# Down projection sums scaled by r and added to h in the output, in place of h divided by r beforehand

## The chip, the cores and the metric

The kernel runs on one core of one Trainium2 chip. The core has TensorE (matrix products; PE and, for its weight loads, PEld in the profile), VectorE (DVE), ScalarE (ACT), GpSimd (POOL) and SyncE (SP). SP and GpSimd issue the DMAs here, each from its own queue in order. The metric is the device time of one execution in microseconds (us).

## The reference

The reference is one decoder layer: 512 tokens behind 16 learned ones, width 2048. What matters here is its second half.

```python
        h = h + o @ w_out[l]

        n2 = _rmsnorm(h, g_ffn[l])
        h = h + (jax.nn.silu(n2 @ w_gate[l]) * (n2 @ w_up[l])) @ w_down[l]

    return h[:, N_META:]
```

`_rmsnorm` multiplies each token with r = 1/sqrt(mean(h*h) + EPS) and each channel with a gain. The inner width of the gate, up and down products is 5632. Since r is one number for each token, it may be applied after a product instead of before: silu(r * (h g) @ w_gate) and r * ((h g) @ w_up), and then the down projection's sum too may take r as a whole.

## The kernel before

All tiles are transposed: 128 channels on the partitions, 512 tokens along the free dimension. The layer runs in stages: input projection, attention and convolution (to about 650 us), output projection with the residual (to 800), gate and up products (800 to 1660), down projection (1660 to the end).

A product in 32-bit precision is made of three passes over operands split into a high and a low part. In the last two stages `pair_product` computes two output tiles for both halves of the tokens at once by a scheme of Strassen's kind: seven block products (numbered 0 to 6) into three PSUM tiles y, z, x (lines 702 to 704). Their weights are prepared by `prepare_pair` under high priority: four weight blocks are loaded by SP (line 591), VectorE adds them up (lines 616, 623, 650), ScalarE casts each of the seven to its high part (609), and VectorE subtracts for the low part (610). Between block products, partial sums are moved out of PSUM: ScalarE copies x, z and x to `sides` (727, 729, 731), and VectorE combines them (733, 737, 740). A PSUM tile can be written again when it was moved out.

**Gate and up.** The loop over f (44 channel tiles of the inner width) runs one `pair_product` each, which gives g1 and u1, and then `gate`: g1 takes r on VectorE (905; r is `r_h`, the tile `acc_h`), silu on ScalarE (906), and the product with u1, which has no r, is made on VectorE, for even f in lines 909 and 910, for odd f in 915 to 918. The results are split (183, 184) and stored to DRAM tiles `fd` through GpSimd's queue (897).

**h and r.** Since u1 lacks r, the down projection's sums lack it as well, and the kernel keeps h / r beside them. The residual stage stores the 16 tiles of h into DRAM tiles `hs[j]`, named hd (line 865). `h_scale` computes r in the first pair, with most of its element-wise work on GpSimd, and `h_inv` = 1/r (499). After the odd f up to 31 a round of `h_over` runs on GpSimd: load a tile of h, multiply it by `h_inv`, store it back (944 to 946).

**Down.** The inner width is split into four chunks of 4, 6, 6 and 6 double tiles. In chunk 0, four pair products make four output tiles each; in chunks 1 to 3, eight make two each. The activations of a chunk are loaded from `fd` into rings through GpSimd's queue (932). In chunks 0 to 2 the sums c1 and c2 are added to `hs` in DRAM by an accumulating DMA of GpSimd's queue:

```python
        gp.dma_start(two(hs[j]), c[:, :, n * T2 :][:, :, :T2], accum_op=ALU.add)
```

for which ScalarE first copies the last block x into c1 (982, 1015). In chunk 3 (`end`) the tiles of `hs` are loaded into `hh` (1000), the sums are added, and the total takes r: c2 on GpSimd (1006, 1007), the two halves of c1 on VectorE (1009 to 1012). SP stores the result to `out` (1008, 1013).

**Order.** A scheduling framework turns this program into one in-order queue for each engine. It simulates the engines with a cost model and takes, of the work that is ready, what stands first in the program; the preparation of weights goes ahead by its high priority. It also sets the waits between queues, from the tiles and tensors that are read and written.

Of the kernel before, what the change touches and what calls it, by code (L numbers as in the profile page):

```python
# [22 lines left out]
KT = D // P  # L23
FT = FF // P

CHUNKS = (4, 6, 6, 6)
# [7 lines left out]
def hybrid_layer(ctx: ExitStack, tc: tile.TileContext, xT, w_in, w_out, w_gu, w_down, vecs, out):  # L34
# [265 lines left out]
    def two(t):  # L300
        return t.rearrange("p (a b) -> p a b", a=2)
# [181 lines left out]
    for h in range(HEADS):  # L483
        head(h)

    def token_scale(acc, dst, count, name, work, inv=None, eng=ve):

        sh, sl, v, y, t = work
        split(sh, sl, acc, eng)
        ps = small(f"ss_{name}")
        pe.matmul(ps, ones_r, sh, start=True, stop=False)
        pe.matmul(ps, ones_r, sl, start=False, stop=True)
        ve.tensor_scalar(v, ps, 1.0 / count, EPS, ALU.mult, ALU.add)
        rsqrt(dst, v, SEQ, y, t, eng)
        if inv is not None:
            eng.tensor_tensor(inv, v, dst, ALU.mult)


    def scale_a():
# [241 lines left out]

    dram = ctx.enter_context(tc.tile_pool(name="dram", bufs=1, space=bass.MemoryType.DRAM))
    fpool = open_pool("fpool", side="right")
    hbuf = open_pool("hbuf", side="right")

    def slots(pool, dt, m, n, name, **kw):

        c = 2 * m * n * T2
        t = pool.tile([P, c + 64], dt, name=name, **kw)
        t = t[:, 4 : 4 + c].rearrange("p (s a k t) -> p s a k t", s=m, a=2, k=n)
        return [t[:, s] for s in range(m)]
# [22 lines left out]
        token_scale(acc_c, acc_c, 1024, "c", w)  # L779

    after(3, scale_c)
    hs = {}
    for i, j in enumerate(OUT_TILES):
        hj = wide_tmp("h", bufs=2)
        gp.dma_start(hj, xT[j][:, META:])
# [75 lines left out]
                    gp.dma_start(fx[s][:, :, k], st[:, :, n])  # L861
        if i < KT - 1:
            square_sum(acc_h, hj, i == 0, wide_tmp("s"))
        hd = dram.tile([P, SEQ], F32, name=f"hd{j}")
        (gp if i < KT - 1 else nc.sync).dma_start(hd, hj)
        hs[j] = hd
    assert not waiting
    acts = [acts[s] for s in range(7)]
    hbuf.release()
# [2 lines left out]
    xyz = open_pool("xyz", 2, space=PSUM)  # L872
    sm = open_pool("sm2", 1, space=PSUM)
    apool = open_pool("apool")
    h_inv = apool.tile([P, SEQ], F32, name="h_inv")

    def h_scale():
        w = apool.tile([P, 5, SEQ], F32R, tag="s5", name="work_r")
        a, b = apool.tile([P, 2, SEQ], F32, tag="odd", name="work_a"), apool.tile([P, SEQ], F32, tag="even", name="work_b")
        with tc.high_priority(1 << 20):  # L880
            token_scale(acc_h, acc_h, D, "h", (w[:, 0], w[:, 1], a[:, 0], a[:, 1], b), h_inv, gp)

    r_h = two(acc_h)

# [16 lines left out]
    even = [None]  # L901

    def gate(f, g1, u1, x):
        sc.copy(g1[:, 1], x)
        ve.tensor_tensor(g1, g1, r_h, ALU.mult)
        sc.activation(g1, g1, AF.Silu)
        if f % 2 == 0:
            even[0] = even_f = apool.tile([P, 3, T2], F32, tag="even", name=f"even{f}")
            ve.tensor_tensor(even_f[:, 0:3:2], g1, u1, ALU.mult)
            ve.tensor_tensor(even_f[:, 1], even_f[:, 0], even_f[:, 2], ALU.subtract)  # L910
# [23 lines left out]
    for f in range(FT):  # L934
        g1 = apool.tile([P, 2, T2], F32, tag="c1", name=f"g{f}")
        u1 = apool.tile([P, 2, T2], F32, tag="c2", name=f"u{f}")
        x = pair_product(acts, g1, u1, None if f else h_scale)
        if f < FT - 1:
            gate(f, g1, u1, x)
        if f % 2 and f // 2 < KT:  # L940

            j = f // 2
            h_over = apool.tile([P, SEQ], F32, tag="odd", name=f"h_over{j}")
            gp.dma_start(h_over, hs[j])
            gp.tensor_tensor(h_over, h_over, h_inv, ALU.mult)
            gp.dma_start(hs[j], h_over)
        if f == 2 * CHUNKS[0] + 1:
            load_acts(0, 0)
    fpool.release()
# [14 lines left out]
    new_places(6)  # L964
    new_places(7)

    def add_down(j, c, n):
        gp.dma_start(two(hs[j]), c[:, :, n * T2 :][:, :, :T2], accum_op=ALU.add)

    for j in range(KT // 4):  # L970
        for s in range(2 * j - 2, 2 * j) if j else ():
            load_acts(1, s)
        c1, c2 = ((d, d_first)[j % 2][:, m : m + 2] for m in (0, 2))
        x = pair_product([rings[0, s] for s in range(7)], c1, c2)
        if j == KT // 4 - 1:
            first.release()
            rings_p[1] = open_pool("ring_a", side="right")
            for i in (1, 3, 4, 5):
                new_places(i)
            pad(rings_p[1], 160)  # L980
            load_acts(1, 6)
        sc.copy(c1[:, 1], x)
        for n in range(2):
            add_down(4 * j + 2 * n + 1, c2, n)
        for n in range(2):
            add_down(4 * j + 2 * n, c1, n)
    for c in range(1, len(CHUNKS)):
        end = c == len(CHUNKS) - 1
        if end:

            hh = slots(rings_p[1], F32, 1, 6, "hh", tag="ring4")[0]
        for j in range(KT // 2):

            if 1 <= j <= 5:
                load_acts(c + 1, j - 1)
            c1, c2 = (two(d[:, j % 2 * 2 + m]) for m in range(2))
            if end:
                h2 = [hh[:, :, 2 * (j % 3) + m] for m in range(2)]
                for m in (1, 0):
                    gp.dma_start(h2[m], two(hs[2 * j + m]))  # L1000
            x = pair_product([rings[c, s] for s in range(7)], c1, c2)
            if j == KT // 2 - 1:
                for s in (5, 6):
                    load_acts(c + 1, s)
            if end:
                gp.tensor_tensor(c2, c2, h2[1], ALU.add)
                gp.tensor_tensor(c2, c2, r_h, ALU.mult)
                nc.sync.dma_start(two(out[2 * j + 1]), c2)
                ve.tensor_tensor(c1[:, 0], c1[:, 0], h2[0][:, 0], ALU.add)
                ve.tensor_tensor(c1[:, 0], c1[:, 0], r_h[:, 0], ALU.mult)  # L1010
                ve.tensor_tensor(c1[:, 1], x, h2[0][:, 1], ALU.add)
                ve.tensor_tensor(c1[:, 1], c1[:, 1], r_h[:, 1], ALU.mult)
                nc.sync.dma_start(two(out[2 * j]), c1)
            else:
                sc.copy(c1[:, 1], x)
                add_down(2 * j + 1, c2, 0)
                add_down(2 * j, c1, 0)
    rings_p[2].release()
    cpool.release()
    rings_p[1].release()  # L1020
# [58 lines left out]
```

## Time and profile before

| what | value |
|---|---|
| median of 3 runs | 2099.22 us (2098.17 to 2100.97) |
| profiled execution | 2099.6 us |
| its span, first to last instruction | 2097.5 us |
| granted TensorE clock, mean | 0.998 |
| VectorE busy | 1637.8 us (78%) |
| GpSimd busy | 465.5 us (22%) |
| h_over rounds: load, product, store | 16 each; product 1959 ns, mean |
| last chunk on GpSimd, line 1006 | 8 of 1866 ns, mean |
| accumulating DMAs into hd | 48 of 256 KB |

A line of a group gives line, engine, operation, output<-inputs, the tile's shape, the number of them, then busy time and the mean of one in ns, then the idle time ahead of them and what ended it. A line of the waits gives who waited for what: total us, times, longest. A line of the timeline gives start and duration in us, engine, line and operation, and in brackets how long the engine sat idle before it and what it waited for. A row by source line gives how many there were, the minimum, median and maximum in ns, and the first and last start in us. A row of the windows gives the stretch, its length, then the busy us and the number of instructions of PE, PEld, DVE, ACT and POOL, the granted clock, the share of the DMA engines and GB/s.

### The profile page before, as it was taken

To read this page: it belongs to the slowest core of one execution; us is meant where nothing else is said; L and a number is where in the kernel's file an instruction comes from. 1 tells how busy PE (TensorE), PEld (TensorE's weight loads), DVE (VectorE), ACT (ScalarE), POOL (GpSimd) and SP (SyncE) were. 2 spreads that over 40 slices of the span, in tenths; PEclk is the share of its full clock that TensorE was granted. 3 is DMA by queue.
4 is the path that set the end of the run, shared out by engine and by line. 5 is a ranking of instruction groups with operands and counts; after the bars stand their busy time and mean duration, and the time that the engine had idled before them with its cause. 6 is when DMAs were issued, how large, how long until landed. Compare 5 with 4: busy or idle time off the path is not lost.

```text
span 2097.5 us, 39273 instructions
## 1 busy us (share of the span) xinstructions
PE 2064.9 (98%) x16086; PEld 1985.3 (95%) x16086; DVE 1637.8 (78%) x2075; ACT 1018.4 (49%) x1532; POOL 465.5 (22%) x577
## 2 busy tenths in 40 slices
PE   8999999999999998999999999999999999999998
PEld 7999999999998888999999999999999999999998
DVE  8777767533336668899899899899888977778798
ACT  5666666322224434555555555554555544444443
POOL 4111111010104544122122122122011243131322
PEclk9999999999999999999999999999999999999999
DMA  5222222222235666556555565565455899696853
GB/s 174 81 71 81 71 81 72 91 91 91 92 120 156 191 180 227 167 153 204 166 168 176 160 183 174 155 187 163 145 172 166 267 340 343 154 338 158 240 172 111
DMA packets 147795, 342.46 MB, mean 163 GB/s; under 512 B 13136, under 2 KB 62800, under 8 KB 147616
## 3 DMA queue, kind: packets, MB, share of 16 engines
q1 hardware_dynamic: 69472, 216.17, 32.3%
q0 software_dynamic: 78144, 123.79, 21.7%
q8 instruction: 126, 2.06, 0.4%
q14 instruction: 53, 0.43, 0.1%
HBM read 268.60 MB, written 71.30 MB: 162 GB/s over the span
## 4 chain that ended last, share of the span: by engine, by line
PE 78%; DVE 10%; ACT 4%; issue 4%; DMA 2%; POOL 1%; SPq 0%; ACTq 0%; DVEq 0%; POOLq 0%
PE x L702 7%; PE x L704 7%; PE x L703 7%; PE z L702 4%; DVE s L610 4%; PE z L703 4%; PE z L704 4%; PE po L682 3%; PE po L683 3%; PE po L681 3%; ACT s L609 3%; PE y L704 2%; PE y L703 2%; PE y L702 2%; PE pv L169 2%
## 5 line engine op out<-in xcount | busy, mean ns | idle before, releaser
L609 ACT CAST s<-t 128x1024 fp32r<-128x1024 f32 (+1 forms) x288 | 283.2, 983 | 342.5 <-PE z L704 169.2
L610 DVE TENSOR_TENSOR s<-t,s 128x1024 fp32r<-128x1024 f32 (+1 forms) x288 | 334.4, 1161 | 116.6 <-ACT s L609 116.2
L703 PE MATMUL x<-f,s 128*128 128x256 f32 x1408 | 387.5, 275 | 2.3 <-DVE f L184 1.3
L704 PE MATMUL x<-f,s 128*128 128x256 f32 x1408 | 387.4, 275 | 1.7 <-DVE s L610 1.7
L702 PE MATMUL x<-f,s 128*128 128x256 f32 x1408 | 387.4, 275 | 0.2 <-ACT f L183 0.2
L609 ACT CAST s<-b 128x1024 fp32r<-128x1024 f32 (+1 forms) x216 | 212.4, 983 | 156.8 <-PE x L704 151.3
L703 PEld LDWEIGHTS x<-f,s 128*128 128x128 f32 x1408 | 264.3, 188 | 2.7 <-DVE f L184 1.5
L704 PEld LDWEIGHTS x<-f,s 128*128 128x128 f32 x1408 | 264.3, 188 | 1.9 <-DVE s L610 1.9
L702 PEld LDWEIGHTS x<-f,s 128*128 128x128 f32 x1408 | 264.3, 188 | 0.5 <-ACT f L183 0.4
L610 DVE TENSOR_TENSOR s<-b,s 128x1024 fp32r<-128x1024 f32 (+1 forms) x216 | 257.4, 1192 | 2.7 <-ACT s L609 2.2
L138 DVE TENSOR_TENSOR wlo<-raw,whi 128x512 fp32r<-128x512 f32 (+1 forms) x198 | 142.4, 720 | 131.1 <-ACT whi L137 130.5
L897 POOL DMA_DIRECT2D fd<-s x147 | 104.1, 925 | 528.8 <-DVE s L184 527.3
L137 ACT CAST whi<-raw 128x512 fp32r<-128x512 f32 (+1 forms) x198 | 121.3, 614 | 185.4 <-PE pu L171 65.5
L702 PE MATMUL z<-f,s 128*128 128x256 f32 x704 | 195.8, 278 | 7.6 <-ACT sides L729 7.6
L703 PE MATMUL z<-f,s 128*128 128x256 f32 x704 | 193.9, 275 | 0.0
L704 PE MATMUL z<-f,s 128*128 128x256 f32 x704 | 193.9, 275 | 0.0
L616 DVE TENSOR_TENSOR t<-b,b 128x1024 f32<-128x1024 f32 (+1 forms) x144 | 165.5, 1149 | 15.7 <-DMA b<-w_down 11.0
L702 PE MATMUL x<-ring,s 128*128 128x256 f32 x608 | 168.8, 278 | 7.8 <-ACT sides L727 4.0
L704 PE MATMUL x<-ring,s 128*128 128x256 f32 x608 | 167.6, 276 | 0.5 <-DVE s L610 0.5
L703 PE MATMUL x<-ring,s 128*128 128x256 f32 x608 | 167.4, 275 | 0.0
L702 PEld LDWEIGHTS z<-f,s 128*128 128x128 f32 x704 | 132.2, 188 | 10.9 <-ACT sides L729 10.9
L704 PEld LDWEIGHTS z<-f,s 128*128 128x128 f32 x704 | 132.2, 188 | 0.0
(356 smaller groups left out, 5681.0 us busy)
## 6 DMA issues: line engine op xcount, KB each, us to landing
b<-w_gu SPq DMA_DIRECT2D x176, 512.0 KB, 4.0
raw<-w_in SPq DMA_DIRECT2D x92, 512.0 KB, 3.3
fd<-s POOLq DMA_DIRECT2D x147, 256.0 KB, 5.3
b<-w_down SPq DMA_DIRECT2D x96, 384.0 KB, 3.9
ring<-fd POOLq DMA_DIRECT2D x42, 768.0 KB, 15.7
wide<-w_out SPq DMA_DIRECT2D x30, 512.0 KB, 3.8
hd<-d POOLq DMA_DIRECT2D x40, 256.0 KB, 7.5
b<-w_down SPq DMA_DIRECT2D x16, 512.0 KB, 7.7
```

What stands on the lines that cost most here:

```text
L137: sc.copy(hi[:, :c], raw)
L138: ve.tensor_tensor(lo[:, :c], raw, hi[:, :c].bitcast(F32), ALU.subtract)
L609: sc.copy(hi, src)
L610: ve.tensor_tensor(lo, src, hi.bitcast(F32), ALU.subtract)
L616: ve.tensor_tensor(sums[name], a, b, ALU.add)
L681: pe.matmul(ps, hi[:, kk], ah, start=k == 0, stop=False)
L682: pe.matmul(ps, hi[:, kk], al, start=False, stop=False)
L683: pe.matmul(ps, lo[:, kk], ah, start=False, stop=k == 7)
L702: pe.matmul(p, hi[:, kk], act[:, 0, k], start=start and j == k == 0, stop=False, skip_group_check=skip)
L703: pe.matmul(p, hi[:, kk], act[:, 1, k], start=False, stop=False, skip_group_check=skip)
L704: pe.matmul(p, lo[:, kk], act[:, 0, k], start=False, stop=k == n - 1, skip_group_check=skip)
L897: gp.dma_start(fd[c][s][:, :, k], t[:, :, i])
```

## The change

- The residual stage stores h at once into `out[j]`. The DRAM tiles hd, `h_inv` and the sixteen `h_over` rounds are gone.
- In `gate`, u1 takes r on VectorE for the first eight f, which are the activations of chunk 0. The sums of chunk 0 thus have r in them already.
- In chunks 1 to 3 the sums take r on VectorE as they leave `pair_product` (c2 as a whole, c1 in two halves, the second read from PSUM in place of ScalarE's copy), and an accumulating DMA adds them to `out`.
- Only the very last pair is treated otherwise: its two tiles of `out` are loaded, added on VectorE, and stored by SP.
- GpSimd computes nothing in the down projection or for h after r; it issues the DMAs.

```diff
-        if inv is not None:
-            eng.tensor_tensor(inv, v, dst, ALU.mult)
...
-        hd = dram.tile([P, SEQ], F32, name=f"hd{j}")
-        (gp if i < KT - 1 else nc.sync).dma_start(hd, hj)
-        hs[j] = hd
+        (gp if i < KT - 1 else nc.sync).dma_start(out[j], hj)
...
     def gate(f, g1, u1, x):
+        if f < 2 * CHUNKS[0]:
+
+            ve.tensor_tensor(u1, u1, r_h, ALU.mult)
         sc.copy(g1[:, 1], x)
...
-        if f % 2 and f // 2 < KT:
-
-            j = f // 2
-            h_over = apool.tile([P, SEQ], F32, tag="odd", name=f"h_over{j}")
-            gp.dma_start(h_over, hs[j])
-            gp.tensor_tensor(h_over, h_over, h_inv, ALU.mult)
-            gp.dma_start(hs[j], h_over)
...
-    def add_down(j, c, n):
-        gp.dma_start(two(hs[j]), c[:, :, n * T2 :][:, :, :T2], accum_op=ALU.add)
+    def add_down(j, c):
+        gp.dma_start(two(out[j]), c, accum_op=ALU.add)
+
+    def part(c, n):
+        return c[:, :, n * T2 : (n + 1) * T2]
+
+    def down(c1, c2, acts, j, so_far):
+
+        x = pair_product(acts, c1, c2)
+        ve.tensor_tensor(c2, c2, r_h, ALU.mult)
+        if so_far:
+            ve.tensor_tensor(c2, c2, so_far[1], ALU.add)
+            nc.sync.dma_start(two(out[2 * j + 1]), c2)
+        else:
+            add_down(2 * j + 1, c2)
+        for k, src in enumerate((c1[:, 0], x)):
+            ve.tensor_tensor(c1[:, k], src, r_h[:, k], ALU.mult)
+            if so_far:
+                ve.tensor_tensor(c1[:, k], c1[:, k], so_far[0][:, k], ALU.add)
+        if so_far:
+            nc.sync.dma_start(two(out[2 * j]), c1)
+        else:
+            add_down(2 * j, c1)
...
-        for n in range(2):
-            add_down(4 * j + 2 * n + 1, c2, n)
-        for n in range(2):
-            add_down(4 * j + 2 * n, c1, n)
+        for m, c in ((1, c2), (0, c1)):
+            for n in range(2):
+                add_down(4 * j + 2 * n + m, part(c, n))
     for c in range(1, len(CHUNKS)):
-        end = c == len(CHUNKS) - 1
-        if end:
-
-            hh = slots(rings_p[1], F32, 1, 6, "hh", tag="ring4")[0]
         for j in range(KT // 2):
...
-            if end:
-                h2 = [hh[:, :, 2 * (j % 3) + m] for m in range(2)]
-                for m in (1, 0):
-                    gp.dma_start(h2[m], two(hs[2 * j + m]))
-            x = pair_product([rings[c, s] for s in range(7)], c1, c2)
+            so_far = None
+            if c == len(CHUNKS) - 1 and j == KT // 2 - 1:
+
+                hh = slots(rings_p[1], F32, 1, 6, "hh", tag="ring4")[0]
+                so_far = [hh[:, :, n] for n in range(2)]
+                for n in range(2):
+                    gp.dma_start(so_far[n], two(out[2 * j + n]))
+            down(c1, c2, [rings[c, s] for s in range(7)], j, so_far)
...
-            if end:
-                gp.tensor_tensor(c2, c2, h2[1], ALU.add)
-                gp.tensor_tensor(c2, c2, r_h, ALU.mult)
-                nc.sync.dma_start(two(out[2 * j + 1]), c2)
-                ve.tensor_tensor(c1[:, 0], c1[:, 0], h2[0][:, 0], ALU.add)
-                ve.tensor_tensor(c1[:, 0], c1[:, 0], r_h[:, 0], ALU.mult)
-                ve.tensor_tensor(c1[:, 1], x, h2[0][:, 1], ALU.add)
-                ve.tensor_tensor(c1[:, 1], c1[:, 1], r_h[:, 1], ALU.mult)
-                nc.sync.dma_start(two(out[2 * j]), c1)
-            else:
-                sc.copy(c1[:, 1], x)
-                add_down(2 * j + 1, c2, 0)
-                add_down(2 * j, c1, 0)
```

More of the change, by code (lines that the diff above doesn't have):

```diff
@@ L484, in hybrid_layer, with token_scale @@
         head(h)
-    def token_scale(acc, dst, count, name, work, inv=None, eng=ve):
+    def token_scale(acc, dst, count, name, work, eng=ve):
         sh, sl, v, y, t = work
@@ L781, in hybrid_layer @@
     after(3, scale_c)
-    hs = {}
     for i, j in enumerate(OUT_TILES):
@@ L874, in hybrid_layer @@
     apool = open_pool("apool")
-    h_inv = apool.tile([P, SEQ], F32, name="h_inv")
     def h_scale():
@@ L880, in h_scale @@
         with tc.high_priority(1 << 20):
-            token_scale(acc_h, acc_h, D, "h", (w[:, 0], w[:, 1], a[:, 0], a[:, 1], b), h_inv, gp)
+            token_scale(acc_h, acc_h, D, "h", (w[:, 0], w[:, 1], a[:, 0], a[:, 1], b), gp)
     r_h = two(acc_h)
```

## The prediction

> **What bounds the kernel now.** I read the busy line first, then the waits of TensorE stage by stage, then the timeline around each wait.
>
> ```profile
> PE 2064.9 (98%) x16086; PEld 1985.3 (95%) x16086; DVE 1637.8 (78%) x2075; ACT 1018.4 (49%) x1532; POOL 465.5 (22%) x577
> ```
>
> TensorE sets the time, so the change can win only where TensorE stands still because something is late. Two such places repeat. The first is the gate and up stage; these are waits of its window from 860 to 1482 us (total, times, longest):
>
> ```profile
> ACT s L183 <- DVE even L910: 12.2, 11, 1.1
> ...
> PE z L702 <- ACT sides L729: 6.9, 16, 0.4
> ```
>
> Sixteen times TensorE waits for the same copy. How long a pair of products takes there is seen from the copy of line 904, which runs once in each: its number, and its first and last start, in the window 849 to 1470 and then in 1489 to 1640.
>
> ```profile
> L904 ACT COPY g<-x x32: 376/377/378, 850.0 to 1451.5; 128x256 f32<-128x256 f32 x32
> ...
> L904 ACT COPY g<-x x8: 376/377/378, 1490.3 to 1623.6; 128x256 f32<-128x256 f32 x8
> ```
>
> The later window takes 133.3/7 = 19.04 us a pair, with no wait. The earlier one takes 601.5 us for 31 pairs, 11.2 us over 31 x 19.04, and holds 15 of the 16 waits: 0.75 us each. The timeline names the cause. First a pair with the wait:
>
> ```profile
> 873.01 2.20 POOL L945 TENSOR_TENSOR h_over<-h_over,h_inv 128x512 f32<-128x512 f32 x1 [7.39 <-DMA h_over<-hd]
> 873.97 2.33 DVE L610 TENSOR_TENSOR s<-b,s 128x1024 fp32r<-128x1024 f32 x1
> 876.22 0.41 DVE L910 TENSOR_TENSOR even<-even 128x256 f32<-128x256 f32 x1
> 876.67 0.62 ACT L183 CAST s<-even 128x512 fp32r<-128x512 f32 x1 [1.11 <-DVE even L910]
> 877.19 0.37 ACT L729 COPY sides<-z 128x256 f32<-128x256 f32 x1
> 877.61 0.39 PE L702 MATMUL z<-f,s 128*128 128x256 f32 x1 [0.43 <-ACT sides L729]
> ```
>
> Then a pair without GpSimd's product:
>
> ```profile
> 1491.06 0.69 DVE L905 TENSOR_TENSOR g<-g,acc_h 128x512 f32<-128x512 f32 x1
> 1492.32 1.23 DVE L610 TENSOR_TENSOR s<-t,s 128x1024 fp32r<-128x1024 f32 x1 [0.57 <-ACT s L609]
> ...
> 1495.20 1.22 DVE L610 TENSOR_TENSOR s<-b,s 128x1024 fp32r<-128x1024 f32 x1
> 1496.33 0.42 DVE L910 TENSOR_TENSOR even<-even 128x256 f32<-128x256 f32 x1
> ...
> 1497.31 0.37 ACT L729 COPY sides<-z 128x256 f32<-128x256 f32 x1
> ...
> 1498.25 0.28 PE L702 MATMUL z<-f,s 128*128 128x256 f32 x1
> ```
>
> The same subtraction of line 610 takes 2.33 us beside GpSimd's multiplication and 1.22 without it. VectorE is 1.1 us late with line 910, ScalarE stands with line 183 in front of line 729, and TensorE needs line 729 before it may overwrite z. In the calm pair line 729 is done at 1497.68 and needed at 1498.25: 0.57 us of slack.
>
> The second place is the last chunk of the down projection. Its steady pair, and after it one of the chunk before:
>
> ```profile
> 2061.05 0.42 DVE L740 TENSOR_TENSOR d<-y,sides 128x256 f32<-128x256 f32 x1
> 2062.24 1.37 POOL L1007 TENSOR_TENSOR d<-d,acc_h 128x512 f32<-128x512 f32 x1
> 2062.37 2.05 DVE L610 TENSOR_TENSOR s<-t,s 128x768 fp32r<-128x768 f32 x1
> 2064.68 0.95 DVE L650 TENSOR_TENSOR t<-t,b 128x768 f32<-128x768 f32 x1
> 2067.21 0.36 ACT L727 COPY sides<-x 128x256 f32<-128x256 f32 x1
> 2067.63 0.39 PE L702 MATMUL x<-ring,s 128*128 128x256 f32 x1 [0.50 <-ACT sides L727]
> ```
>
> ```profile
> 1940.23 0.42 DVE L740 TENSOR_TENSOR d<-y,sides 128x256 f32<-128x256 f32 x1
> 1941.10 0.96 DVE L610 TENSOR_TENSOR s<-t,s 128x768 fp32r<-128x768 f32 x1 [0.45 <-ACT s L609]
> 1942.09 0.96 DVE L650 TENSOR_TENSOR t<-t,b 128x768 f32<-128x768 f32 x1
> 1944.01 0.96 DVE L610 TENSOR_TENSOR s<-t,s 128x768 fp32r<-128x768 f32 x1 [0.96 <-ACT s L609]
> ...
> 1944.35 0.84 ACT L609 CAST s<-b 128x768 fp32r<-128x768 f32 x1 [0.38 <-PE x L704]
> 1945.09 0.36 ACT L727 COPY sides<-x 128x256 f32<-128x256 f32 x1
> ...
> 1946.15 0.28 PE L702 MATMUL x<-ring,s 128*128 128x256 f32 x1
> ```
>
> From line 740 to line 650 VectorE needs 3.63 us in the last chunk and 1.86 before. Line 650 feeds a cast that stands ahead of line 727 on ScalarE. The slack is the 0.38 us that the cast of line 609 sat idle, and 0.70 from the end of line 727 (1945.45) to its use at 1946.15: 1.08 us in all. A delay of 1.77 overruns it.
>
> What the chunk loses is counted from once-a-pair rows: line 727 in chunk 2, line 727 in chunk 3, and line 740 from the last pair of chunk 2 to the end.
>
> ```profile
> L727 ACT COPY sides<-x x4: 364/364/364, 1916.5 to 1959.4; 128x256 f32<-128x256 f32 x4
> ...
> L727 ACT COPY sides<-x x7: 364/364/365, 1991.7 to 2082.3; 128x256 f32<-128x256 f32 x7
> ...
> L740 DVE TENSOR_TENSOR d<-y,sides x9: 418/425/425, 1970.3 to 2091.2; 128x256 f32<-128x256 f32 x9
> ```
>
> That is 14.30 us a pair (42.9/3) against 15.10 (90.6/6): 0.80 more. Over eight pairs line 740 takes 120.9 us where 8 x 14.30 = 114.4 would do: 6.5 us lost.
>
> **The change, part by part.**
>
> *The rounds of h are gone* (load, product and store on GpSimd's queue, sixteen times, with the one product for h_inv, whose first reader is the 873.01 row). The late subtraction, and with it sixteen waits of 0.75, should go: **-12.0 us**. Whoever doubts that needs another cause for waits that end where these products end; the window from 1489 has the same code but for them. The bound on the other side is 0. The store of h goes through the same queues as before to another address: nothing.
>
> *u times r in the first eight products.* One 128x512 multiplication on VectorE, priced by line 905: 0.69 us. Its input is ready well before line 905 needs its own, and VectorE sits idle for 0.57 us between lines 905 and 610, so 0.12 may remain. The bound is all of it, 8 x 0.69 = 5.5, and below 0 nothing speaks for a gain. Only the four even products carry the critical cast behind line 910; were the idle time missed, each would stall 0.69 - 0.57 = 0.12 us. The first of the eight may also wait a little for r itself. I take **+0.4 us**.
>
> *Products with r in chunks 1 and 2* (16 pairs). New on VectorE: one 128x512 (0.69) and two 128x256 (0.42 each, from line 740): 1.53 us, while ScalarE loses the copy of line 1015. The idle times quoted for chunk 2, 0.45 and 0.96, hold nearly that. What counts is the delay of line 650: the whole multiplication and one half ahead of it make 1.11 - 0.45 = 0.66 us, under the slack of 1.08; with the other half too it is 1.08, just at the edge. So the steady pairs cost nothing. A pair in which VectorE waits for a weight load lacks the 0.45 us of idle time: 1.11 or 1.53 against 1.08, at most 0.45 us late. About five pairs at the chunks' starts are so; I take **+0.8 us**. Bounds: 0, and 16 x 0.80 = 12.8 if each pair stalls as in chunk 3.
>
> The accumulations now wait for VectorE's last half instead of ScalarE's copy, and loads for the next chunk stand behind them on GpSimd's queue. The half starts some 0.7 us later than the copy did; the loads serve the next chunk, so this costs nothing, and 0.7 us at each of two chunk starts if they were last.
>
> *Chunk 3.* GpSimd's two products a pair go, and with them the doubled line 610; VectorE's own four halves become the 1.53 us of chunks 1 and 2. So it should run at their 14.30. Of the 6.5 us lost, 6 x 0.80 = 4.8 are the steady stall. The rest is in its first two pairs, where a weight load is late too:
>
> ```profile
> 1970.40 2.15 POOL L1000 DMA_DIRECT2D hh<-hd  x3
> ...
> 1983.35 0.96 DVE L616 TENSOR_TENSOR t<-b,b 128x768 f32<-128x768 f32 x1 [1.37 <-DMA b<-w_down]
> ...
> 1975.00:1980.00 5.00, 5.00 (x47) 5.00 (x46) 4.20 (x5) 2.39 (x5) 0.00 (x0) 1.00 1.06 334
> ```
>
> The DMA engines are full (share 1.06) just before, and six loads of h were issued into that; seven of the eight pairs load no h any more. I take the whole **-6.5 us**; the low end is -4.8.
>
> *The last pair.* Two 128x512 operations come from GpSimd to VectorE:
>
> ```profile
> 2091.25 0.42 DVE L740 TENSOR_TENSOR d<-y,sides 128x256 f32<-128x256 f32 x1 [1.61 <-PE y L704]
> ...
> 2094.20 0.33 SPq L1013 DMA_DIRECT2D out_T<-d  x1
> ```
>
> 2 x 0.69 = 1.38 fits into the 1.61 us of idle time ahead of line 740; behind the last matmul stand two halves and a store on SP, as before: 0. Without that cover it would be 1.4.
>
> **The sum:** 2099.6 (the profiled execution: 2097.5 of span and 2.1 around it) - 12.0 + 0.4 + 0.8 - 6.5 = 2082.3. That execution lies 0.4 above the median of the runs, so on their scale **2082**.
>
> **The rivals.**
>
> *The products with r use up the slack* in every pair of chunks 1 to 3, because all three land ahead of line 650 and a little more. Then 16 pairs lose 0.80, and chunk 3 gains only 6.5 - 4.8 = 1.7: 2099.6 - 12.0 + 0.4 + 12.8 - 1.7 = 2099, no change. For it: 1.08 against 1.08 in the worst order. Against: that order needs x's half, ready only after the pair's last matmul, ahead of line 650.
>
> *Chunk 3 alone gains nothing* beyond that 1.7, as VectorE works there as much as before: 2099.6 - 12.0 + 1.2 - 1.7 = 2087. Against it: of the 1.77 us of delay, 1.1 is the doubled line 610.
>
> *Slower: the accumulations wait for one another.* They now all write one tensor. If order is kept over the whole of it, not by its rows, each waits on GpSimd's queue until the one before has landed (KB, then us to landing):
>
> ```profile
> hd<-d POOLq DMA_DIRECT2D x40, 256.0 KB, 7.5
> ...
> hd<-d_first POOLq DMA_DIRECT2D x8, 256.0 KB, 13.3
> ```
>
> Chunk 0 has 8 of each, 166 us in line against four pairs of some 19: 90 late, 38 of it covered as buffers are reused two pairs later, so +52; afterwards two a pair, 15.0 against 14.3, +0.7 x 23 = 16: 2150. It decides from a landing of half a pair, 7.1 us, on. If only the same row must wait, its last access is eight pairs, 114 us, old, and nothing waits. The Trainium skill, "DMA: Bandwidth & Descriptors", section "Rules for kernel authors", says that an accumulating DMA reads its destination and writes it later, so that any other access of the same bytes has to wait for its semaphore; that speaks for waits by row and asks none between rows. No trace here shows which it is.
>
> **How the numbers follow.** The forecast has 0.79, with its own range 2078 to 2088 (all of both gains and no cost gives 2080.7 on the median's scale; chunk 3 at its low end with 3 us of small stalls 2086). No change has 0.07, chunk 3 without gain 0.08, slower 0.06. The range 2077 to 2092 leaves out the first and the last of these rivals. A measurement of this kernel tells about 0.2%, 4.2 us: faster 0.88 (the forecast, chunk 3 without gain and a little of the first rival), same 0.06, slower 0.06.
>
> **What would show it.** Line 904 should come every 19.04 us from the second product to the last, with no wait for line 729; line 610 of form 128x768 should stay at 0.96 us in chunk 3 and line 740 come every 14.3. Waits for line 727 in chunks 1 and 2 would show the first rival, waits of GpSimd's queue for a landing on the output the last. A pair of 19.8 us without any product on GpSimd would prove the reading of the first stage wrong.

## The result and the profile after

The kernel after takes 2083.55 us in the median of three executions (2082.79 to 2085.22; a fourth, disturbed one of 7323.63 us is left out), the kernel before 2100.09 beside it. The ratio is 0.992, with a 95% interval of 0.9898 to 0.9941, so the gain of 0.8% is small but clear of the scatter. The profiled execution takes 2083.55 us with a span of 2081.8, against 2099.6 and 2097.5 before. So the span is 15.7 us shorter, where the forecast's terms make 17.3.

The first part of the page after:

```profile
PE 2056.5 (99%) x16086; PEld 1982.3 (95%) x16086; DVE 1634.6 (79%) x2126; ACT 1014.7 (49%) x1516; POOL 389.2 (19%) x512
```

VectorE is as busy as before (1637.8), GpSimd less by 76 us. In the changed kernel the line numbers are smaller: the copy 904 is 902, the subtraction 610 is 608, the add 616 is 614, 650 is 648, the copy 727 is 725, the combinations 737 and 740 are 735 and 738. Rows by source line, after: the once-a-pair copy in gate and up from the second product on, and the new product of u1 (seven of its eight fall into that window).

```profile
L902 ACT COPY g<-x x41: 376/376/378, 847.3 to 1608.9; 128x256 f32<-128x256 f32 x41
...
L901 DVE TENSOR_TENSOR u<-u,acc_h x7: 691/692/693, 843.1 to 957.4; 128x512 f32<-128x512 f32 x7
```

That is 761.6/40 = 19.04 us a pair throughout. Before, the same stretch ran from 850.0 to 1623.6 by the rows of line 904: 773.6, or 12.0 more. The timeline of VectorE shows why the product of u1 (0.69 us) costs nothing: it sits in the first part of the pair, and the idle time of 0.57 us further on is still there.

```profile
862.72 0.69 DVE L901 TENSOR_TENSOR u<-u,acc_h 128x512 f32<-128x512 f32 x1
...
867.19 0.68 DVE L903 TENSOR_TENSOR g<-g,acc_h 128x512 f32<-128x512 f32 x1
868.45 1.23 DVE L608 TENSOR_TENSOR s<-t,s 128x1024 fp32r<-128x1024 f32 x1 [0.57 <-ACT s L607]
```

Chunk 3 by line 725, and line 738 from the last pair of chunk 2 to the end:

```profile
L725 ACT COPY sides<-x x7: 358/363/365, 1980.9 to 2066.5; 128x256 f32<-128x256 f32 x7
...
L738 DVE TENSOR_TENSOR d<-y,sides x9: 414/414/425, 1961.0 to 2076.0; 128x256 f32<-128x256 f32 x9
```

A pair takes 85.6/6 = 14.27 us here (15.10 before); counted from TensorE's first product of one pair to that of the next, 14.28. Line 738 spans 115.0 us where line 740 spanned 120.9: 5.9 less.

The loss is in chunks 1 and 2. The copy has 23 instances in chunks 1 to 3; without any stall the 22 intervals would take 22 x 14.28 = 314.2 us. What the copy's row spans beyond 314.2 is called the loss of the chunks, here and for every kernel below. The row before:

```profile
L727 ACT COPY sides<-x x23: 360/364/365, 1755.7 to 2082.3; 128x256 f32<-128x256 f32 x23
```

and after:

```profile
L725 ACT COPY sides<-x x23: 358/363/368, 1741.1 to 2066.5; 128x256 f32<-128x256 f32 x23
```

The loss is 326.6 - 314.2 = 12.4 us before and 11.2 after. Of the 12.4, about 4.9 were the steady stall of chunk 3 (six intervals of 0.82), so 7.5 lay at the starts of the chunks. After, all 11.2 lie there. Put together by the same rows:

| stretch | forecast | measured, us |
|---|---|---|
| span's start to gate and up's second product (850.0; 847.3) | none | -2.7 |
| gate and up (773.6; 761.6) | -12.0 + 0.4 | -12.0 |
| chunk 0 (1623.6 to 1755.7; 1608.9 to 1741.1) | 0 | +0.1 |
| chunks 1 and 2 (1755.7 to 1970.3; 1741.1 to 1961.0) | +0.8 | **+5.3** |
| chunk 3 (120.9; 115.0) | -6.5 | -5.9 |
| behind the last line 740 or 738 (6.3; 5.8) | 0 | -0.5 |

One term is off by far. Here are the rows of such a chunk start: VectorE in the second pair of chunk 1, from one add that waits for a late weight load to the same add of the next pair, and below it the row of SP's queue (start of the first of three weight loads, then the time to the end of the third's issue). Before:

```profile
1763.67 0.96 DVE L616 TENSOR_TENSOR t<-b,b 128x768 f32<-128x768 f32 x1 [0.80 <-DMA b<-w_down]
...
1767.07 0.96 DVE L650 TENSOR_TENSOR t<-t,b 128x768 f32<-128x768 f32 x1
...
1770.86 0.95 DVE L610 TENSOR_TENSOR s<-b,s 128x768 fp32r<-128x768 f32 x1
...
1774.45 0.96 DVE L616 TENSOR_TENSOR t<-b,b 128x768 f32<-128x768 f32 x1 [1.01 <-DMA b<-w_down]
...
1778.47 0.96 DVE L616 TENSOR_TENSOR t<-b,b 128x768 f32<-128x768 f32 x1 [0.99 <-DMA b<-w_down]
...
1764.66 7.51 SPq L591 DMA_DIRECT2D b<-w_down  x3
```

After:

```profile
1749.56 0.96 DVE L614 TENSOR_TENSOR t<-b,b 128x768 f32<-128x768 f32 x1 [1.33 <-DMA b<-w_down]
...
1751.64 0.68 DVE L967 TENSOR_TENSOR d<-d,acc_h 128x512 f32<-128x512 f32 x1
...
1752.69 0.42 DVE L974 TENSOR_TENSOR d<-d,acc_h 128x256 f32<-128x256 f32 x1
...
1754.02 0.96 DVE L648 TENSOR_TENSOR t<-t,b 128x768 f32<-128x768 f32 x1
...
1757.82 0.95 DVE L608 TENSOR_TENSOR s<-b,s 128x768 fp32r<-128x768 f32 x1
...
1761.36 0.96 DVE L614 TENSOR_TENSOR t<-b,b 128x768 f32<-128x768 f32 x1 [1.72 <-DMA b<-w_down]
...
1765.30 0.96 DVE L614 TENSOR_TENSOR t<-b,b 128x768 f32<-128x768 f32 x1 [0.91 <-DMA b<-w_down]
...
1750.55 8.58 SPq L589 DMA_DIRECT2D b<-w_down  x3
```

From line 616 to line 650 VectorE needs 3.40 us before; from 614 to 648 it needs 4.46. The 1.06 are the new products of c2 and of c1's first half. The subtraction of a loaded block further on (1770.86, line 610; 1757.82, line 608) is as late, and SP's third load waits for it: in both kernels it is issued as that subtraction ends, after 8.58 - 7.51 = 1.07 us more. From its issue it takes about as long as before to land, 6.4 us (6.5 before), and the last add shown waits for it. So VectorE, SP's issue and the landing form a round, from the first of these rows to the last: 14.80 us before, 15.74 after, where TensorE needs 14.28.

The wait in between, 1.72 us instead of 1.01, is not part of that round. It is for the second of the three loads, which in both kernels is issued some 2.2 us behind the first row, before the new products can delay it; it landed after 9.5 us instead of 8.5. In a second profile of the kernel after (r_after below) the same wait is 0.62 us, and the round takes 15.75 all the same.

The wait ends in TensorE. In the last pair of chunk 2 it stands 2.11 us for line 735, which is behind a line 614 that waited 2.89 us for its load, and afterwards the granted clock is halved for one stretch (timeline, then windows):

```profile
1959.73 0.36 PE L700 MATMUL x<-ring,s 128*128 128x256 f32 x1 [2.11 <-DVE d L735]
```

```profile
1957.00:1959.70 2.70, 0.62 (x6) 0.42 (x4) 1.41 (x3) 0.83 (x1) 0.00 (x0) 1.00 1.11 393
...
1961.00:1962.00 1.00, 1.00 (x6) 1.00 (x6) 0.97 (x4) 0.00 (x0) 0.64 (x1) 0.50 1.08 393
...
1964.00:1966.00 2.00, 2.00 (x19) 2.00 (x19) 1.32 (x3) 0.81 (x2) 0.00 (x0) 1.00 0.72 148
```

So three causes were possible for the 5.3 us: VectorE's added work, the accumulations issued later (and the bursts of loads behind them, with a DMA share of 1.11), and the halved clock.

### The profile page after: what moved, and what is told of

The parts are those of the page before. It is cut to its first block, busy times and chain, and to the rows that moved or that the text cites. A ratio compares the mean times of both kernels' runs of the same rounds, so it can differ in the third digit from the quotient of the medians.

```text
span 2081.8 us, 39149 instructions
## 1 busy us (share of the span) xinstructions
PE 2056.5 (99%) x16086; PEld 1982.3 (95%) x16086; DVE 1634.6 (79%) x2126; ACT 1014.7 (49%) x1516; POOL 389.2 (19%) x512
## 4 chain that ended last, share of the span: by engine, by line
PE 93%; DVE 4%; DMA 2%; ACT 1%; issue 1%; SPq 0%; DVEq 0%; ACTq 0%
PE x L700 11%; PE x L702 11%; PE x L701 11%; PE z L700 5%; PE z L701 5%; PE z L702 5%; PE y L700 3%; PE y L702 3%; PE y L701 3%; PE po L681 3%; PE po L679 3%; PE po L680 3%; PE pv L169 2%; PE pu L173 1%; PE pc L173 1%; PE pu L169 1%
## 5 line engine op out<-in xcount | busy, mean ns | idle before, releaser
L608 DVE TENSOR_TENSOR s<-t,s 128x1024 fp32r<-128x1024 f32 (+1 forms) x288 | 326.7, 1134 | 102.5 <-ACT s L607 100.5
L608 DVE TENSOR_TENSOR s<-b,s 128x1024 fp32r<-128x1024 f32 (+1 forms) x216 | 246.3, 1140 | 2.4 <-ACT s L607 1.7
L614 DVE TENSOR_TENSOR t<-b,b 128x1024 f32<-128x1024 f32 (+1 forms) x144 | 165.8, 1152 | 17.3 <-DMA b<-w_down 12.7
```

The source lines that it names most:

```text
L608: ve.tensor_tensor(lo, src, hi.bitcast(F32), ALU.subtract)
L614: ve.tensor_tensor(sums[name], a, b, ALU.add)
```

## The experiments

| kernel | time, us (median) | ratio to before, 95% interval | loss of the chunks, us |
|---|---|---|---|
| after | 2083.55 | 0.992 (0.9898 to 0.9941) | 11.2 |
| e1_no_h_product | 2086.51 | 0.9947 (0.9932 to 0.9962) | 13.2 |
| e9_no_c2_products | 2094.35 | 0.9967 (0.9954 to 0.9981) | 7.7 |
| e2_x_by_scalar | 2083.65 | 0.9931 (0.9916 to 0.9946) | 10.3 |
| e3_x_alone | 2081.47 | 0.9916 (0.9899 to 0.9932) | 5.6 |
| e5_fill | 2082.76 | 0.9924 (0.9909 to 0.9939) | 9.9 |
| e10_spare_products | 2085.59 | 0.9928 (0.9912 to 0.9943) | 9.8 |
| e11_c2_late | 2081.12 | 0.9911 (0.9896 to 0.9926) | 6.5 |
| e6_all_u | 2080.89 | 0.9902 (0.9887 to 0.9916) | 5.6 |
| e7_rings_held | 2082.03 | 0.9904 (0.9887 to 0.992) | 7.7 |
| e8_all_u_held | 2078.65 | 0.9893 (0.9878 to 0.9908) | 5.2 |
| r_after | 2086.94 | 0.9933 (0.9919 to 0.9947) | 10.6 |
| r_all_u_held | 2079.91 | 0.9901 (0.9887 to 0.9915) | 5.6 |

The times of one kernel scatter by some us, in part ahead of the chunks (below), so a difference of 3 us is read from the rows of the profile and not from the medians. Each loss is from one profile; those of two profiles of the same kernel differ by 0.6 us (after and r_after) and 0.4 (e8 and r_all_u_held).

**The product for h alone** (the kernel before, with one line less):

```diff
-            gp.tensor_tensor(h_over, h_over, h_inv, ALU.mult)
```

> The kernel before, with line 945 alone left out: the sixteen tiles of h are still loaded and stored back in the gate and up stage, but not multiplied by h_inv (the output then lacks that division). If GpSimd's product beside VectorE's subtraction makes the sixteen waits, line 904 comes every 19.04 us through the whole stage, line 610 stays at 1.22 us, and the time falls by 16 x 0.75 = 12 to about 2088. If instead the loads and stores of the round, or the round's place in the order, make them, pairs of 19.8 us remain and the time stays above 2095.

Line 904 of this kernel:

```profile
L904 ACT COPY g<-x x32: 376/377/378, 847.3 to 1437.6; 128x256 f32<-128x256 f32 x32
```

590.3/31 = 19.04 us in every pair, with all loads and stores of the round still there. The first theory holds; the rounds' DMAs cost nothing.

**The products of chunk 3 on GpSimd** (the kernel before, without lines 1006 and 1007):

```diff
-                gp.tensor_tensor(c2, c2, h2[1], ALU.add)
-                gp.tensor_tensor(c2, c2, r_h, ALU.mult)
```

> The kernel before, with lines 1006 and 1007 alone left out: in chunk 3 GpSimd computes nothing, while its loads of h, the four operations of VectorE on c1 and the stores stay (c2's tiles are stored without h and r). If the products on GpSimd beside VectorE make the 0.80 us of stall in each pair, the steady pairs of chunk 3 come every 14.28 us instead of 15.10, line 610 takes 0.96 us, and the time falls by 4.8 to 6.5 us to about 2093. If VectorE's own four operations or the loads of h make it, the pairs stay at 15.1 and the time at 2098 to 2099.

Rows of chunk 3:

```profile
L727 ACT COPY sides<-x x7: 360/362/363, 1996.4 to 2082.0; 128x256 f32<-128x256 f32 x7
...
L610 DVE TENSOR_TENSOR s<-t,s x28: 952/958/960, 1992.6 to 2088.2; 128x768 fp32r<-128x768 f32 x28
```

85.6/6 = 14.27 us a pair, and line 610 at 0.96: the steady stall of 0.8 came from GpSimd's products beside VectorE, not from VectorE's own four operations, which are still there. The loads of h are there too, and with them a late weight load at the start of the chunk, a single wait of 2.4 us:

```profile
DVE t L616 <- DMA b<-w_down: 2.4, 1, 2.4
```

In the kernel after, VectorE has no such wait behind the first pair of that chunk. The profiled execution of this kernel took 2099.43 us, against a median of 2094.35, for a reason outside the chunks: it reaches gate and up's second product at 854.6, the kernel before at 850.0, with the same code up to there.

**ScalarE copies x's half** (in chunks 1 and 2):

```diff
-            ve.tensor_tensor(c1[:, k], src, r_h[:, k], ALU.mult)
+            if k and c < len(CHUNKS) - 1:
+                sc.copy(c1[:, k], src)
+            else:
+                ve.tensor_tensor(c1[:, k], src, r_h[:, k], ALU.mult)
```

> The kernel after, except that in chunks 1 and 2 ScalarE copies x's half into c1, as in the kernel before, and that half is not multiplied by r there (a quarter of those chunks' sums lacks r). The products of c2 and of c1's first half stay on VectorE. Theory: the last accumulation of a chunk is issued too late behind VectorE's last half, the next chunk's loads and with them the weight loads land later, TensorE waits over 2 us at the chunk's start, and its clock then halves for 3.4 us. Then the first pairs of chunks 2 and 3, now 18.0 and 18.3 us, go back to about 15.5, no window of half the clock is left there, and the time falls by some 5.5 to about 2079. Rival, VectorE's added work itself delays the chunk's start: two of three products are left, so the first pairs stay above 17 us and the time above 2082.

```profile
L725 ACT COPY sides<-x x23: 360/363/366, 1741.0 to 2065.5; 128x256 f32<-128x256 f32 x23
```

The loss is 324.5 - 314.2 = 10.3 us, hardly less, and 2083.65 us is no gain that can be told. The theory with which this run was made, the late accumulation of c1, falls: that accumulation goes out behind ScalarE's copy again, and the loss stays.

**x's half alone takes r** (in chunks 1 and 2):

```diff
-        ve.tensor_tensor(c2, c2, r_h, ALU.mult)
+        if c == len(CHUNKS) - 1:
+            ve.tensor_tensor(c2, c2, r_h, ALU.mult)
...
+            if k or c == len(CHUNKS) - 1:
+                ve.tensor_tensor(c1[:, k], src, r_h[:, k], ALU.mult)
```

> The kernel after, except that in chunks 1 and 2 only x's half takes r: c2 and the first half of c1 are left without it (three quarters of those chunks' sums lack r). VectorE has 1.1 us less to do in each pair, but the last accumulation still waits for VectorE's last half. Theory of the late accumulation: the first pairs of chunks 2 and 3 stay at 17.5 to 18.5 us, each with a window of half the clock, and the time stays within 2 us of the kernel after (2083 to 2086). Rival, VectorE's added work is what delays: the pairs fall to about 15.5, and the time to about 2079.

```profile
L725 ACT COPY sides<-x x23: 358/363/367, 1746.5 to 2066.3; 128x256 f32<-128x256 f32 x23
...
1755.53 7.52 SPq L589 DMA_DIRECT2D b<-w_down  x3
```

319.8 - 314.2 = 5.6 us: the rival holds. Without the products of c2 and of c1's first half the chunk starts lose no more than before (7.5), and SP's third load comes after 7.52 us again.

**Work without anyone waiting for it, and waiting without work.** Those two products do two things: they fill VectorE, and they hold c2's accumulation back. The first kernel writes them to a spare tile; the second leaves them out and makes the accumulation wait for line 738 by a copy of one element (both change only chunks 1 and 2, and both keep x's half).

```diff
+        end = c == len(CHUNKS) - 1
+        spare = None if end else two(small(f"spare{c}_{j}"))
-        ve.tensor_tensor(c2, c2, r_h, ALU.mult)
+        ve.tensor_tensor(c2 if end else spare, c2, r_h, ALU.mult)
...
-            ve.tensor_tensor(c1[:, k], src, r_h[:, k], ALU.mult)
+            ve.tensor_tensor(c1[:, k] if end or k else spare[:, k], src, r_h[:, k], ALU.mult)
```

```diff
-        ve.tensor_tensor(c2, c2, r_h, ALU.mult)
+        end = c == len(CHUNKS) - 1
+        if end:
+            ve.tensor_tensor(c2, c2, r_h, ALU.mult)
+        else:
+            ve.tensor_copy(c2[0:1, 1, 0:1], c1[0:1, 0, 0:1])
...
-            ve.tensor_tensor(c1[:, k], src, r_h[:, k], ALU.mult)
+            if end or k:
+                ve.tensor_tensor(c1[:, k], src, r_h[:, k], ALU.mult)
```

> The kernel after, except that in chunks 1 and 2 the products of c2 and of c1's first half are made in the same order on VectorE but written to a spare tile that nobody reads; c2 and that half go into the sums without r (three quarters of those sums lack it). Only x's half is still multiplied in place. VectorE thus works as much as in the kernel after, while the accumulation of c2 waits for nothing of it. Summed over the nine pairs of the chunks' starts (the second to fourth of chunk 1, the last of chunk 1 with three of chunk 2, the last of chunk 2 with one of chunk 3), the loss over 14.28 us a pair is 11.3 us in the kernel after and 5.6 in the one with x's half alone. If VectorE's work makes the difference, it is 10 to 11 us here too, and the time 2083 to 2085. If the later accumulation of c2 makes it, it is 5 to 6.5 us, and the time about 2079 to 2081.

> The other way round: the kernel with x's half alone multiplied in chunks 1 and 2, and a copy of one element on VectorE behind line 738 that c2's accumulation has to wait for, so that it is issued some 1.2 us later, about where the kernel after issues it, with next to no work for VectorE (three quarters of those chunks' sums lack r, and one element of each c2 is overwritten). If VectorE's work makes the loss at the chunks' starts, it stays at 5 to 6.5 us and the time at 2079 to 2081. If the later accumulation makes it, it is 10 to 11 us and the time 2083 to 2085.

The spare products:

```profile
L725 ACT COPY sides<-x x23: 358/363/367, 1744.9 to 2068.9; 128x256 f32<-128x256 f32 x23
...
1754.65 8.59 SPq L589 DMA_DIRECT2D b<-w_down  x3
```

The late accumulation:

```profile
L725 ACT COPY sides<-x x23: 358/363/365, 1742.5 to 2063.2; 128x256 f32<-128x256 f32 x23
...
1751.59 7.70 SPq L589 DMA_DIRECT2D b<-w_down  x3
```

9.8 us of loss and 8.59 with the work, 6.5 and 7.70 with the waiting, against 11.2 and 8.58 in the kernel after and 5.6 and 7.52 with neither. Of the 5.6 us between the last two, VectorE's work alone makes 4.2 and the later accumulation alone 0.9. The 4.2 is clear of the scatter between two profiles, the 0.9 hardly. The medians go the same way, 2085.59 and 2081.12 on one chip.

The round of the second pair, and the stretch of chunks 1 and 2 as in the table of the forecast, divide these kernels in the same way:

| kernel | round, us | chunks 1 and 2, us over before |
|---|---|---|
| before | 14.80 | |
| after; r_after | 15.74; 15.75 | +5.3; +6.4 |
| e10_spare_products (the work) | 15.71 | +5.5 |
| e11_c2_late (the waiting) | 14.72 | +1.6 |
| e3_x_alone (neither) | 14.78 | +0.7 |

The work alone is enough for the longer round and for all of the +5.3.

**The clock** (ten matmuls in the wait):

```diff
+        if i in (FT + KT // 4 + KT // 2 - 1, FT + KT // 4 + KT - 1):
+            fill = small(f"fill{i}")
+            for n in range(10):
+                pe.matmul(fill[:, :T2], ones_r, acts[6][:, 0, 0], start=True, stop=True)
```

> The kernel after, with ten more matmuls of 128x256 (some 1.1 us) into a spare PSUM tile, ahead of the last block product in the last pair of chunks 1 and 2, where TensorE waits over 2 us for weights. The result is the same. If the wait of over 2 us is what halves the clock afterwards, the wait is now about 1 us, the clock stays at full speed, each of the two chunk starts loses the 1.7 us that the half clock costs, and the time falls by about 3.4 to 2081. If the clock falls there for another cause, the windows of half the clock stay and the time is the same, or up to 2 us longer.

```profile
1957.70 1.35 PE L741 MATMUL fill<-ring,ones_r 128*128 128x256 f32 x10
...
1960.48 0.35 PE L700 MATMUL x<-ring,s 128*128 128x256 f32 x1 [1.44 <-DVE d L735]
```

```profile
1957.50:1960.50 3.00, 1.56 (x15) 1.39 (x13) 1.46 (x3) 0.84 (x1) 0.00 (x0) 1.00 1.12 402
1960.50:1963.50 3.00, 3.00 (x26) 3.00 (x27) 2.93 (x5) 0.00 (x0) 0.92 (x1) 1.00 0.98 288
```

The clock stays at full speed, but the loss is still 9.9 us, not the 7.8 that 11.2 less 3.4 would be, and the time is 2082.76, not 2081. Nor does this run show that the matmuls kept the clock, as the kernel after run once more shows.

> The kernel after once more, for a second profile of the chunks' starts and beside the kernel with u1 times r for all f and the loads held. Gate and up come every 19.04 us again, chunk 3 every 14.28, the loss at the chunks' starts is 10 to 11.5 us; whether the clock is halved in the waits there depends on where they fall, so 0 to 2 such windows. What differs from the first profile by more than 1 us is the first pair of gate and up, where one load lands early or late. About 2084.

```profile
1961.18 0.36 PE L700 MATMUL x<-ring,s 128*128 128x256 f32 x1 [2.33 <-DVE d L735]
...
1961.00:1963.00 2.00, 1.82 (x16) 1.85 (x17) 1.97 (x5) 0.00 (x0) 0.20 (x1) 1.00 1.14 406
```

```profile
L725 ACT COPY sides<-x x23: 358/363/365, 1741.5 to 2066.3; 128x256 f32<-128x256 f32 x23
```

The same kernel, a wait of 2.33 us, longer than the 2.11 of the first profile, and the clock isn't halved at all. The loss is 10.6 us, only 0.6 below that of the profile with the halved clock. The profiles of e2_x_by_scalar and e10_spare_products have no halved clock in the chunks either, with losses of 10.3 and 9.8. So most of the loss is there without the halved clock.

**The way out** that these runs point to is to multiply earlier. All u1 take r in gate and up, where the 0.69 us cost nothing, and the sums of the down projection need no r:

```diff
-        if f < 2 * CHUNKS[0]:
-            ve.tensor_tensor(u1, u1, r_h, ALU.mult)
+        ve.tensor_tensor(u1, u1, r_h, ALU.mult)
...
-        ve.tensor_tensor(c2, c2, r_h, ALU.mult)
...
-            ve.tensor_tensor(c1[:, k], src, r_h[:, k], ALU.mult)
...
+            sc.copy(c1[:, 1], x)
```

> The kernel after, but u1 takes r for all 44 f (36 more multiplications of 128x512 on VectorE, 0.69 us each), so that no sum of the down projection has to: the products of chunks 1 to 3 are gone, ScalarE copies x's half as before, and in the last pair only the sum with the loaded tiles is left. The result is the same. The runs so far say that with the products on VectorE the weight load at a chunk's start is issued 0.4 us later and lands up to 1.2 later, and that VectorE then works off its lag over one to three pairs; if that is so, the three chunk starts return to the kernel before's (14.6 and 14.8 in chunk 1, 15.6, 15.2 and 15.1 in chunk 2, about 16 in chunk 3), no clock is halved, gate and up stay at 19.04 us a pair, and the time falls by 4 to 6 us to about 2079. If the multiplications fill VectorE in gate and up, pairs above 19.1 us appear there, and each 0.1 us of them costs 3.6 us in all.

```profile
L900 ACT COPY g<-x x42: 372/375/375, 849.2 to 1629.8; 128x256 f32<-128x256 f32 x42
...
L725 ACT COPY sides<-x x23: 359/362/364, 1743.2 to 2063.0; 128x256 f32<-128x256 f32 x23
```

780.6/41 = 19.04 us a pair in gate and up, and a loss of 5.6 us in the chunks: 2080.89 us.

The other idea was to keep the loads of the next chunk's last two activations behind the weight load:

```diff
+            if hold is not None:
+                ve.tensor_copy(rings[c, s][0:1, :, 0, 0:1], hold[0:1, 0, 0:2].unsqueeze(2))
...
+        if j == KT // 2 - 1:
+            for s in (5, 6):
+                load_acts(c + 1, s, c2)
```

> The kernel after, with the loads of the last two activations of the next chunk (four of 768 KB) held until VectorE's line 731 of a chunk's last pair (by a copy of two elements into their buffer), so that the weight load of the next pair lands ahead of them. The result is the same. If the weight load's late landing in the burst of those loads makes the wait at the chunk's start, it lands about 4 us earlier, the first pairs of chunks 2 and 3 fall from 18.0 and 18.3 to 14.3 to 15.0, no clock is halved there, and the time falls by 5 to 8 us to about 2078. If VectorE's work itself is the bound there, or the activations now come too late for the next chunk, waits stay or appear in the pair behind, and the time stays above 2082.

> Both of the last two edits in the kernel after: u1 takes r for all f, and the loads of the last two activations of the next chunk are held until line 731. The result is the same. If the late weight load and VectorE's lag are two independent parts of the chunk starts, this is the fastest of all, with chunk starts of 14.3 to 14.8 us and about 2075; if one of them alone makes the loss, it is no faster than the better of the two.

> The kernel with u1 times r for all f and the loads of the last two activations held, once more, beside the kernel after on the same chip. If both edits are worth what their profiles show (some 6 us at the chunks' starts), it is 5 to 6 us faster than the kernel after, about 2078.5; if the first time had only fewer disturbed first pairs, the two come within 2 us.

Held loads alone, then both edits together:

```profile
L725 ACT COPY sides<-x x23: 358/363/367, 1746.7 to 2068.6; 128x256 f32<-128x256 f32 x23
```

```profile
L725 ACT COPY sides<-x x23: 362/364/365, 1741.0 to 2060.4; 128x256 f32<-128x256 f32 x23
```

Alone, the hold lowers the loss to 321.9 - 314.2 = 7.7 us, and the time is 2082.03, not the 2078 expected if the burst alone made the wait. With u1 times r it is 5.2 (5.6 in the second run), against 5.6 for u1 times r alone: the hold adds next to nothing, so the two are not independent parts. The faster median of the two together, 2078.65 against 2080.89, isn't shown to come from it. On one chip beside the kernel after, u1 times r with the hold takes 2079.91 and the kernel after 2086.94 us: 7.0 us less. It beats both kernels.

**What scatters.** Beside the forecast's stretches the first 850 us gave 2.7 us. The kernel without the product for h shows that h_inv isn't the cause: it still computes h_inv and reaches its second product at 847.3, as the kernel after does. In part it is one load that lands late in the first pair, and TensorE's wait for it is another in each profile: 1.0 us in the kernel before, none after, 3.5 in the kernel where x's half alone takes r.

```profile
829.73 0.39 PE L703 MATMUL x<-f,s 128*128 128x256 f32 x1 [1.03 <-DMA f<-fx]
```

```profile
PE x L701 <- DMA f<-fx: 3.5, 1, 3.5
```

The rest, over 1 us, was ahead of this stage already and wasn't traced further. That it is scatter is seen from three profiles with the same code up to the second product: the kernel before reaches it at 850.0, the kernel without the product for h at 847.3, the one without the products of chunk 3 at 854.6.

## Why the prediction was right, and where it was wrong

The time, the sign and the likeliest case came out as forecast; of the terms, the two gains are right in size and cause, one is too small by 4.5 us, and by luck an unforecast 2.7 us of scatter made up for part of it.

- *Gate and up, -12.0.* Measured -12.0, and shown to be GpSimd's multiplication beside the subtraction: without that one line every pair takes 19.04 us.
- *u times r, +0.4.* Measured 0, for eight products and for 44. The product has its own place early in the pair; the 0.12 us by which it seemed to overrun the idle time didn't come.
- *Chunk 3, -6.5.* Measured -5.9 (-7.6 in the second profile, where chunks 1 and 2 measure +6.4: the border between the stretches lies in a late pair). The steady part is shown to be the two products on GpSimd. For the rest, the late weight load in the second pair, the loads of h were named. The run that keeps these loads keeps the wait, and the kernel after has neither; a run that drops the loads alone wasn't made.
- *Chunks 1 and 2, +0.8, the mis-sized term.* The prediction had the steady pairs at nothing, and that is right: 14.28 us. The step that failed is "A pair in which VectorE waits for a weight load lacks the 0.45 us of idle time: 1.11 or 1.53 against 1.08, at most 0.45 us late." It measured +5.3. The comparison of 1.11 with the slack was made for one pair, with the weight load's own time fixed. But the lag of 1.06 reaches the subtraction behind line 648 that sets free the buffer of the next weight load. That load goes out 1.07 us later and takes 6.4 us to land, so the add that waits for it in the next pair is late by nearly as much: 15.74 us for the round in place of 14.80. The two such pairs at the start of chunk 2 lengthen by 0.73 and 0.50 us (15.19 to 15.92 and 15.00 to 15.50), as the lag goes round from load to VectorE to load. That the work makes it is shown: alone it makes 4.2 of 5.6 us of loss, moves the third load's issue to 8.59 and the round to 15.71.
- *The accumulations, "costs nothing, and 0.7 us at each of two chunk starts if they were last".* About right: making c2's accumulation late by itself adds 0.9 us in all, hardly more than two profiles of one kernel differ by.
- *The last pair, 0.* The cover held: line 738 still waits for TensorE, with 0.16 us of the 1.61 left, and the last store is issued 2.95 us behind it, as before. What was saved lies behind that issue.

```profile
2075.96 0.42 DVE L738 TENSOR_TENSOR d<-y,sides 128x256 f32<-128x256 f32 x1 [0.16 <-PE y L702]
```


*The rivals.* The products using up the slack in every pair: refuted, since pairs outside the chunks' starts take 14.3 us, in chunk 3 as above and in chunk 2 too (57.2/4 by this row of line 725).

```profile
L725 ACT COPY sides<-x x5: 358/362/363, 1891.1 to 1948.3; 128x256 f32<-128x256 f32 x5
```

Chunk 3 without gain: refuted by -5.9. The accumulations waiting for one another: refuted. In the waits of GpSimd's queue through chunks 1 to 3, after, the accumulations wait for VectorE's results; only the load of the last pair waits for a landing on the output, once, and hidden. (In chunk 0 one accumulation waits 0.8 us for another to land; the kernel before, with a tensor for each tile, has such a wait of 1.8 us there.)

```profile
POOL out_T L959 <- DVE d L967: 199.8, 21, 11.9
POOL out_T L959 <- DVE d L974: 53.2, 22, 11.1
POOL hh L1010 <- DMA out_T<-d: 5.9, 1, 5.9
```

The Trainium skill's rule that the prediction weighed ("DMA: Bandwidth & Descriptors", "Rules for kernel authors") asks for a wait by bytes, and the trace agrees: 5.9 us once, for the rows that are read back, and none between rows in these chunks.

## What to carry to other kernels

Where an engine frees the buffer that a load waits for, work put ahead of that instruction delays the next load too, and comparing it with one pair's slack undercounts it wherever loads already land late. The time to compare with TensorE's is the whole round, from the freeing of the buffer over issue and landing to the next freeing: 1.06 us of added work a pair became 4.2 us over the chunk starts. If a factor can be applied at several places, put it where the engine's idle time lies clear of the loads; here the multiplication by r cost nothing in gate and up and some 5 us in the down projection. And a total that agrees should be checked by stretches: here an error of 4.5 us and 2.7 us of scatter stood against each other.

## What was not expected of the hardware

TensorE waits of 1.85 and 2.11 us (in the last pairs of chunks 1 and 2) were each followed by about 3.4 us at a granted clock of 0.50, while those of 2.47 and 2.33 us at the same places in another execution of the same kernel were not. So the length of the wait alone doesn't decide it. The Trainium skill, "TensorE: Matmul & The Clock Gate", section "What's actually happening", says that activity is judged in windows of about 3.4 us which run freely, and that the clock falls back after at least one idle window. The length of the slow stretch agrees, and freely running windows would let a wait that falls into one window count where one split over two does not; but a wait clearly shorter than a whole window was enough here, which differs from the page. No run moved the wait on purpose to test it.

The halved clock also cost less than its arithmetic. At half speed 3.4 us do the work of 1.7, yet the two profiles of the kernel after, one with two such stretches and one with none, differ by 0.6 us of loss: while TensorE was slow, VectorE had time to work off its lag. That last sentence is an inference from the total; no run shows it by itself.
